# A two-layer streaming encoder step: norm weights applied on ScalarE, last tiles squared singly, two blocks normed before the SSM, roots by table

## The chip, the cores and the metric

One core of a Trainium2 chip runs one step of a small streaming encoder. The metric is the device time of one execution in microseconds (us), here the median of several runs. The core has a matrix engine (PE, TensorE, which reads SBUF and writes PSUM banks), three elementwise engines (DVE, VectorE; ACT, ScalarE, which looks its functions up in tables that it loads; POOL, GpSimd), and a sync engine (SP) that issues most DMAs in the order of its own queue. Each engine runs its instructions in order and waits at semaphores for the others.

## The reference

Two layers over T = 1088 tokens (1024 of a prompt, 64 of a sample), width 1024, fp32. Every block is sandwiched between norms, and this change is about them.

```python
def rms_norm(x, g):
    x32 = x.astype(jnp.float32)
    y = x32 * lax.rsqrt(jnp.mean(x32 * x32, axis=-1, keepdims=True) + NORM_EPS) * g.astype(jnp.float32)
...
def conv_ffn(h, prev, w_up, conv_w, conv_b, w_down):
    up = h @ w_up
    full = jnp.concatenate([prev.astype(up.dtype), up], axis=1)
    c = conv_b
    for j in range(CONV_WIDTH):
        c = c + conv_w[j] * full[:, j:j + t]
    y = (jax.nn.gelu(c[..., :D_FF]) * c[..., D_FF:]) @ w_down
...
    for i in range(DEPTH):
        hp = rms_norm(xp, g_pre_mix[i])
...
        xp = xp + rms_norm(mp, g_post_mix[i])
...
        hp = rms_norm(xp, g_pre_ffn[i])
...
        xp = xp + rms_norm(fp, g_post_ffn[i])
```

The mixer of layer 0 is windowed attention. That of layer 1 is an SSM: an input matrix, a complex diagonal scan over tokens, an output matrix, GELU, and a gated product (GLU).

## The kernel before

**Layout.** Activations lie transposed: 128 partitions, 8 k-tiles of the width, tokens along the free axis. The tokens are cut into blocks of 384, 384 and 320 (b = 0, 1, 2). A product of fp32 values is three matmuls (`mm3`, L181 to L183) of high and low halves: of the activations (`hh`, `hl`) and the weights (`whl`). Weights come by SP's DMA into `raw`, ACT rounds them to the high half (L175), DVE subtracts for the low half (L176), two units ahead of use.

**Stages.** Attention, FFN 0, SSM, FFN 1. Between them lie the joints, where a post norm adds to the residual and a pre norm makes the next input: J1 (post_norm 1, pre_norm 2), J3 (post_norm 3, SSM norm), J4 (post_norm 5, pre_norm 6) and the end, J5 (post_norm 7 and the output); J2 is where FFN 0 turns from up to down. Block 2 is last at each joint. J3 and J5 stand alone, since nothing else is left for PE; in J1 and J4 PE works on the up products of blocks 0 and 1 while block 2 is normed.

**A norm** (`rstd`, L186). ACT squares two k-tiles at a time (L196), DVE adds them up (L198) and folds the pair (L201), PE sums over partitions with a column of ones (L207). The root is either by ACT's Sqrt (L211), a reciprocal and one Newton step on DVE (L230 to L232), or, with `root` false (J4), a bit trick and three Newton steps on DVE (L217 to L232), because Sqrt needs another table than the stage's sigmoid. PE then transposes the factors into a broadcast row `pr` (L225). `post_norm` multiplies `y` by weight and `pr` in one instruction for each k-tile on DVE (L264) and adds the residual, two k-tiles at a time, on POOL or DVE (L266). `pre_norm` makes `hh` on ACT (L241), `hl` on DVE (L247) or for k = 3, 5, 7 on POOL (L245), and `rb` (L249), which scales the up products as they leave PSUM (L295).

**Up** has 88 units of one weight tile: a buffer `u` is taken from the pool `t4`, two of its columns copied from a cache (L286), filled from PSUM, two more columns kept (L300), and run through the width-3 convolution on ACT and DVE (L303 to L305). **Down** (`down`) holds four PSUM banks, one for each of four output tiles, and goes over k; ACT empties them (L392) or DVE adds them (L394).

**Into the SSM.** `ssm_bounce` copies the new residual into `xs` with tokens reordered by position in a chunk of 8 (L867, ACT); blocks 0 and 1 during down of block 2, block 2 in J3. The four quarters go to DRAM (`hd`, L873) and come back as `U` (L917), 16 channels of a group on the partitions. The factors of the norm are applied then, by DVE on `U` for all 137 columns (`ssm_scale`, L923): `ssm_norm` spreads them with small products (L902) into `rs`. The SSM runs over 32 pairs, `batch` after `batch`: PE forms inputs (L990), DVE multiplies and scans (L991 to L1013), PE forms outputs (L1028), ACT drains them (`ys`, L1032).

**What sets the order.** The program is written in tiles; a framework's scheduler, which simulates the program, puts the instructions of each engine in one fixed order, within the limits of tile pools and of explicit order constraints (`order`). So an edit can move instructions far from it.

## Time and profile before

| what | us |
|---|---|
| median of 3 runs | 2345.57 (2342.53 to 2351.72) |
| profiled execution | 2347.37 |
| its span in the trace | 2345.6 |
| PE busy | 2267.0 |
| DVE busy | 1460.2 |
| ACT busy | 893.7 |
| POOL busy | 277.5 |

The profiled execution is 1.8 us above the median, and its span is 1.8 us shorter than its own time. The timeline rows read: start in us from the span's start, busy us, engine, line and operation, outputs<-inputs, shape, count, and in brackets the idle time ahead of it with what ended it. A PE row merges pipelined matmuls.

### The profile page before, as it was taken

How to read it: one execution, taken by the hardware profiler on the slowest of the kernel's cores; microseconds unless marked ns; L12 is line 12 of the kernel's file. 1: busy time of each engine (PE TensorE's matmuls, PEld its weight loads, DVE VectorE, ACT ScalarE, POOL GpSimd, SP SyncE). 2: the span in 40 equal slices, each digit the busy share in tenths (PEclk: the TensorE clock that was granted, in tenths of full speed). 3: DMA queues.
4: the chain of work that ended last, by engine and by line, in shares of the span. 5: the costliest groups of instructions: out<-in, count | busy, mean ns of one | idle time of the engine just before them, and what ended most of it. 6: DMA issues, size and time to landing. Idle time of an engine off the chain costs nothing. (4 is left out here: it accounts for less than half of the span.)

```text
span 2345.6 us, 35751 instructions
## 1 busy us (share of the span) xinstructions
PE 2267.0 (97%) x14265; PEld 2197.5 (94%) x14265; DVE 1460.2 (62%) x2836; ACT 893.7 (38%) x1463; POOL 277.5 (12%) x286
## 2 busy tenths in 40 slices
PE   8999999999999999999968899999999999999997
PEld 7987799999999999999956799999999999999997
DVE  8677639898576766564649712587555555465554
ACT  5256645322233433443625621343222222254332
POOL 5222005000123221010000000240000000000000
PEclk9999999999999999999978899999999999999998
DMA  5000015312334344765567721242211221166652
GB/s 191 33 30 19 28 51 176 118 62 102 97 127 144 126 139 150 230 193 162 193 250 243 222 68 54 73 155 82 93 60 71 85 74 64 56 215 182 208 179 94
DMA packets 167958, 287.01 MB, mean 122 GB/s; under 512 B 22032, under 2 KB 104496, under 8 KB 167664
## 3 DMA queue, kind: packets, MB, share of 16 engines
q1 hardware_dynamic: 157440, 273.41, 35.8%
q0 software_dynamic: 2032, 6.83, 0.9%
q10 hardware_dynamic: 8320, 4.49, 0.8%
q8 instruction: 112, 1.84, 0.3%
q14 instruction: 54, 0.44, 0.1%
HBM read 214.52 MB, written 70.17 MB: 121 GB/s over the span
## 5 line engine op out<-in xcount | busy, mean ns | idle before, releaser
L181 PE MATMUL mm<-hl,whl 128*128 128x384 f32 (+1 forms) x2232 | 735.1, 330 | 16.0 <-DVE hl L247 7.5
L183 PE MATMUL mm<-hh,whl 128*128 128x384 f32 (+1 forms) x2232 | 733.4, 329 | 1.9 <-DVE whl L176 1.9
L182 PE MATMUL mm<-hh,whl 128*128 128x384 f32 (+1 forms) x2232 | 734.9, 329 | 0.0
L175 ACT ACTIVATE whl<-raw 128x1024 fp32r<-128x1024 f32 x256 | 269.9, 1058 | 709.6 <-PE mm L183 583.5
L176 DVE TENSOR_TENSOR whl<-raw,whl 128x1024 fp32r<-128x1024 f32 x256 | 320.7, 1255 | 232.5 <-ACT whl L175 229.7
L181 PEld LDWEIGHTS mm<-hl,whl 128*128 128x128 f32 x2232 | 420.3, 188 | 18.1 <-DVE hl L247 9.0
L183 PEld LDWEIGHTS mm<-hh,whl 128*128 128x128 f32 x2232 | 420.1, 188 | 2.8 <-DVE whl L176 2.7
L182 PEld LDWEIGHTS mm<-hh,whl 128*128 128x128 f32 x2232 | 420.5, 188 | 0.4
L181 PE MATMUL mm<-gt,whl 128*128 128x384 f32 (+1 forms) x1056 | 347.0, 329 | 3.6 <-ACT y L392 2.8
L182 PE MATMUL mm<-gt,whl 128*128 128x384 f32 (+1 forms) x1056 | 345.9, 328 | 0.0
L183 PE MATMUL mm<-gt,whl 128*128 128x384 f32 (+1 forms) x1056 | 343.1, 328 | 0.7 <-DVE whl L176 0.7
L295 DVE TENSOR_TENSOR u<-rb,mm 128x384 f32<-128x384 f32 (+1 forms) x264 | 131.8, 507 | 284.6 <-PE mm L183 283.5
L181 PEld LDWEIGHTS mm<-gt,whl 128*128 128x128 f32 x1056 | 198.7, 188 | 4.9 <-ACT y L392 3.4
L183 PEld LDWEIGHTS mm<-gt,whl 128*128 128x128 f32 x1056 | 198.3, 188 | 1.0 <-DVE whl L176 1.0
L182 PEld LDWEIGHTS mm<-gt,whl 128*128 128x128 f32 x1056 | 198.9, 188 | 0.0
L303 ACT ACTIVATE t<-u,ppt 128x1090 f32<-128x1090 f32 x88 | 113.4, 1289 | 29.3 <-DVE u L297 17.7
L304 DVE SCALAR_TENSOR_TENSOR t<-u,ppt,t 128x1090 f32<-128x1090 f32 x88 | 118.9, 1351 | 7.9 <-ACT t L303 7.9
L305 DVE SCALAR_TENSOR_TENSOR t<-u,ppt,t 128x1090 f32<-128x1090 f32 x88 | 118.9, 1351 | 1.7
L266 POOL TENSOR_TENSOR y<-y,xl 128x768 f32<-128x768 f32 (+1 forms) x18 | 32.3, 1801 | 624.6 <-DVE y L264 409.3
L318 ACT ACTIVATE t<-t 128x1090 f32<-128x1090 f32 x44 | 49.0, 1114 | 101.3 <-DVE t L305 101.3
L1085 DVE SCALAR_TENSOR_TENSOR y<-pa,ppt,sg 128x384 f32<-128x384 f32 (+1 forms) x24 | 14.1, 592 | 95.5 <-ACT sg L1084 95.5
L370 DVE TENSOR_TENSOR gt<-gr,gt 128x768 fp32r<-128x768 f32 (+2 forms) x70 | 57.9, 864 | 17.5 <-ACT gt L369 17.5
(315 smaller groups left out, 3279.1 us busy)
## 6 DMA issues: line engine op xcount, KB each, us to landing
raw<-in_w_down SPq DMA_DIRECT2D x132, 512.0 KB, 4.0
raw<-in_w_up SPq DMA_DIRECT2D x88, 512.0 KB, 3.3
gd<-t SPq DMA_DIRECT2D x44, 512.0 KB, 2.6
pm<-prm SPq DMA_DIRECT2D x32, 522.0 KB, 7.1
gr<-gd SPq DMA_DIRECT2D x28, 384.0 KB, 4.8
xl<-x SPq DMA_DIRECT2D x24, 384.0 KB, 4.0
raw<-in_w_glu SPq DMA_DIRECT2D x16, 512.0 KB, 4.4
gr<-gd SPq DMA_DIRECT2D x22, 320.0 KB, 4.6
```

The source lines that it names most:

```text
L175: nc.scalar.activation(w[:, 0], raw, AF.Copy)
L176: nc.vector.tensor_sub(w[:, 1], raw, w[:, 0].bitcast(F32))
L181: nc.tensor.matmul(out, w[:, 0, sl], xl, start=start, stop=False)
L182: nc.tensor.matmul(out, w[:, 0, sl], xh, start=False, stop=False)
L183: self.last_mm = nc.tensor.matmul(out, w[:, 1, sl], xh, start=False, stop=stop)
L266: by[q].tensor_add(y[:, 2 * q:2 * q + 2], y[:, 2 * q:2 * q + 2], xs[q])
L295: nc.vector.tensor_mul(u[:, t0 + 2:t0 + 2 + np_], rb[:, t0:t0 + np_], ps[:, :np_])
L303: nc.scalar.activation(t, u[:, 0:T + 2], AF.Identity, bias=cb(m), scale=cw(0, m))
L304: nc.vector.scalar_tensor_tensor(t, u[:, 1:T + 3], cw(1, m), t, op0=ALU.mult, op1=ALU.add)
L305: nc.vector.scalar_tensor_tensor(t, u[:, 2:T + 4], cw(2, m), t, op0=ALU.mult, op1=ALU.add)
L318: nc.scalar.activation(ta, ta, AF.Gelu_apprx_tanh)
L370: nc.vector.tensor_sub(x[:, 1, j:j + e], raw, x[:, 0, j:j + e].bitcast(F32))
```

## The change

Seven edits, all in the norms and what stands beside them:

1. `rstd` with `fine` (post norms of block 2): the last pair of k-tiles is squared and added one at a time, and the accumulator is folded before it.
2. `post_norm`: ACT scales `y` by the weight in eight activations (L269), ahead of the root; DVE multiplies pairs of k-tiles by `pr` (L277). Which engine adds the residual is a string, 0 for POOL and 1 for DVE: in block 2, "1111" for post_norm 3, "0101" for all others. In block 2 a product stays behind the DVE add ahead of it.
3. The roots of J4 come from the table for block 2 of post_norm 5 and blocks 1 and 2 of pre_norm 6.
4. The two small copies of each up unit go from DVE to ACT.
5. In `down`, the second half (mh = 1) of the first pass (c = 0) takes banks 0 and 1 for its first four k, and then banks 2 and 3.
6. The SSM norm of blocks 0 and 1 is applied before the bounce: `pr` is broadcast as in the other norms, kept in `rn`, and DVE multiplies in place of ACT's copy. `ssm_scale` covers only the 41 columns of block 2.
7. The order constraint of block 2's copies: the second copy stands behind the second square instead of the third.

```diff
--- before.py
+++ after.py
@@ -183,13 +183,20 @@
         self.last_mm = nc.tensor.matmul(out, w[:, 1, sl], xh, start=False, stop=stop)
 
 
-    def rstd(self, src, n, tag, root, bcast=True, first=False, alt=None, adder=None):
+    def rstd(self, src, n, tag, root, bcast=True, first=False, alt=None, adder=None, fine=False):
         nc = self.nc
         adder = adder or nc.vector
         acc = None
         for q in range(4):
             sq = self.n2(n, tag)
             xq = src[:, 2 * q:2 * q + 2]
+            if fine and q == 3:
+                adder.tensor_add(acc[:, 0], acc[:, 0], acc[:, 1])
+                for j in range(2):
+                    nc.scalar.activation(sq[:, j], xq[:, j], AF.Square)
+                    adder.tensor_add(acc[:, 0], acc[:, 0], sq[:, j])
+                break
             if first:
                 nc.gpsimd.tensor_mul(sq, xq, xq)
             else:
@@ -198,7 +205,8 @@
                 adder.tensor_add(acc, acc, sq)
             else:
                 acc = sq
-        self.summed = adder.tensor_add(acc[:, 0], acc[:, 0], acc[:, 1])
+        else:
+            adder.tensor_add(acc[:, 0], acc[:, 0], acc[:, 1])
         cuts = [min(c, n - P) for c in range(0, n, P)]
         nt = len(cuts)
         pr = self.sm_ps("pr", int(tag == "sqb") if alt is None else alt)
@@ -249,23 +257,31 @@
         nc.scalar.activation(rb[:, t0:t0 + n], pr[:, :n], AF.Copy)
         return hh, hl, r
 
-    def post_norm(self, y, b, g, xsrc, root, roomy, out=None):
+    def post_norm(self, y, b, g, xsrc, root, roomy, out=None, by=None):
 
         nc = self.nc
         n = BLK[b][1]
         xs = [self.t4([P, 2, n], "xl") if roomy and b == 2 else self.n2(n, "xl") for _ in range(4)]
         for q in range(4):
             nc.sync.dma_start(xs[q], xsrc[:, 2 * q:2 * q + 2])
-        pr, _ = self.rstd(y, n, "sqa", root, alt=b % 2 if roomy else None)
+        pr, _ = self.rstd(y, n, "sqa", root, alt=b % 2 if roomy else None, fine=b == 2)
+        for k in range(KD):
+            nc.scalar.activation(y[:, k], y[:, k], AF.Copy, scale=g[:, k:k + 1])
+        V, G = nc.vector, nc.gpsimd
+        by = [(G, V)[int(x)] for x in by or ("1001" if roomy and b == 2 else "0101")]
 
         def apply():
+            last = None
             for q in range(4):
-                for k in range(2 * q, 2 * q + 2):
-                    nc.vector.scalar_tensor_tensor(y[:, k], y[:, k], g[:, k:k + 1], pr[:, :n], op0=ALU.mult, op1=ALU.mult)
-                by = (nc.vector, nc.gpsimd, nc.gpsimd, nc.vector) if roomy and b == 2 else (nc.gpsimd, nc.vector) * 2
-                by[q].tensor_add(y[:, 2 * q:2 * q + 2], y[:, 2 * q:2 * q + 2], xs[q])
+                yq = y[:, 2 * q:2 * q + 2]
+                x = V.tensor_mul(yq, yq, pr[:, None, :n].to_broadcast([P, 2, n]))
+                if last is not None and b == 2:
+                    self.order(x, last)
+                x = by[q].tensor_add(yq, yq, xs[q])
+                if by[q] is V:
+                    last = x
                 if out is not None:
-                    nc.sync.dma_start(out[:, 2 * q:2 * q + 2], y[:, 2 * q:2 * q + 2])
+                    nc.sync.dma_start(out[:, 2 * q:2 * q + 2], yq)
         return apply
 
 
@@ -283,7 +299,7 @@
             u = self.t4([P, T + 4], "u")
             nc.vector.memset(u[:, 0:2], 0.0)
...
-            nc.vector.tensor_copy(u[:, SEQ + 2:SEQ + 4], self.pp[:, c0:c0 + 2])
+            nc.scalar.copy(u[:, SEQ + 2:SEQ + 4], self.pp[:, c0:c0 + 2])
...
 
...
@@ -297,8 +313,8 @@
                 nc.vector.tensor_mul(u[:, SEQ + 4:], rb[:, SEQ:], ps[:, np_:n])
 
         def conv(m, u):
-            nc.vector.tensor_copy(cst[:, m], bass.AP(tensor=u.tensor, offset=u[:, SEQ:SEQ + 2].offset,
-                                                     ap=[u.ap[0], [T + 2 - SEQ, 2], [1, 2]]))
+            nc.scalar.copy(cst[:, m], bass.AP(tensor=u.tensor, offset=u[:, SEQ:SEQ + 2].offset,
+                                                ap=[u.ap[0], [T + 2 - SEQ, 2], [1, 2]]))
             t = self.t4([P, T + 2], "t")
             nc.scalar.activation(t, u[:, 0:T + 2], AF.Identity, bias=cb(m), scale=cw(0, m))
             nc.vector.scalar_tensor_tensor(t, u[:, 1:T + 3], cw(1, m), t, op0=ALU.mult, op1=ALU.add)
@@ -380,6 +396,9 @@
                 ks = range(KCUT[c], KCUT[c + 1])
...
                 todo = [(k, m) for m in range(4) for k in ks] if ws else [(k, m) for k in ks for m in range(4)]
+                if c == 0 and mh == 1:
+                    todo = [(k, m) for u in ((0, 1), (2, 3)) for k in ks[:4] for m in u] + todo[16:]
                 for k, m in todo:
...
                         ws[k] = self.unit(("w_down", i, k, mh))
@@ -851,8 +870,7 @@
     def ssm_bounce(self, xt, b, qs=range(4), after=None):
 
         nc = self.nc
-        t0, n = BLK[b]
-        segs = [(0, n, 48 * b)] if b < 2 else [(0, 256, 96), (256, 320, 129)]
+        segs = [(0, 384, 48 * b)] if b < 2 else [(0, 256, 96), (256, 320, 129)]
         if b == 0:
             self.hw = {}
             self.hd = self.dram.tile([D, 8, NC_], F32, name="hd")
@@ -864,9 +882,14 @@
                 o = self.xs[q][:, :, :, c:c + (v - u) // 8]
...
-                x = nc.scalar.activation(o, xt[:, 2 * q:2 * q + 2, u:v].rearrange("p k (c s) -> p k c s", s=8), AF.Copy)
+                x = xt[:, 2 * q:2 * q + 2, u:v].rearrange("p k (c s) -> p k c s", s=8)
+                if b < 2:
+                    r = self.rn[:, 384 * b:384 * b + 384].rearrange("p (c s) -> p c s", s=8)
+                    nc.vector.tensor_mul(o, x, r[:, None].to_broadcast([P, 2, 48, 8]))
+                    continue
+                x = nc.scalar.activation(o, x, AF.Copy)
                 if after is not None:
-                    self.order(x, after[(0, 2, 3, 3)[q]])
+                    self.order(x, after[(0, 1, 3, 3)[q]])
             if b == 2:
...
@@ -882,29 +905,29 @@
 
         nc = self.nc
         n = BLK[b][1]
-        ps, r = self.rstd(xt, n, "sqa" if b == 2 else "sqb", True, bcast=False, alt=1 - b % 2, adder=nc.gpsimd if b == 0 else None)
+        ps, r = self.rstd(xt, n, "sqa" if b == 2 else "sqb", True, bcast=b < 2, alt=1 - b % 2, adder=nc.gpsimd if b == 0 else None)
         if b == 0:
...
-            sel = self.t4([P, 330], "sel")
-            self.lsel, self.dsel, self.ex, self.rs = sel[:, :128], sel[:, 128:144], sel[:, 144:192], sel[:, 192:329]
+            sel = self.t4([P, 1001], "sel")
+            self.lsel, self.dsel, self.ex, self.rs, self.rn = (sel[:, x:y] for x, y in ((0, 128), (128, 144), (144, 192), (192, 233), (233, 1001)))
...
-            nc.vector.memset(self.rs[:, 128:129], 0.0)
+            nc.vector.memset(self.rs[:, 32:33], 0.0)
+        if b < 2:
+            nc.scalar.activation(self.rn[:, 384 * b:384 * b + 384], ps[:, :n], AF.Copy)
+            return
         ex = self.ex
         for i, c in enumerate(range(0, n, P)):
...
-        if b < 2:
-            self.last_rs = nc.scalar.activation(self.rs[:, 48 * b:48 * b + 48], ps[:, :48], AF.Copy)
-        else:
-            nc.scalar.activation(self.rs[:, 96:128], ps[:, :32], AF.Copy)
-            self.last_rs = nc.scalar.activation(self.rs[:, 129:137], ps[:, 32:40], AF.Copy)
+        nc.scalar.activation(self.rs[:, 0:32], ps[:, :32], AF.Copy)
+        self.last_rs = nc.scalar.activation(self.rs[:, 33:41], ps[:, 32:40], AF.Copy)
 
     def ssm_load(self, q):
 
@@ -920,7 +943,9 @@
         return u
 
     def ssm_scale(self, u, x, y):
-        return self.nc.vector.tensor_mul(u[:, x:y], u[:, x:y], self.rs[:, None, :].to_broadcast([P, y - x, NC_]))
+        u = u[:, x:y, 96:]
+        return self.nc.vector.tensor_mul(u, u, self.rs[:, None, :].to_broadcast([P, y - x, 41]))
 
     def ssm(self, after):
         nc, tc, a = self.nc, self.tc, self.a
@@ -1194,7 +1219,8 @@
 
             def f(b, y):
                 ys.append(y)
-                c.post_norm(y, b, g(post), xs[b], post != 5, post in (3, 7), xo[b] if pre is None else None)()
+                c.post_norm(y, b, g(post), xs[b], post != 5 or b == 2, post in (3, 7), xo[b] if pre is None else None,
+                            {3: "1111", 7: "0101"}.get(post) if b == 2 else None)()
                 if pre == 4:
                     if b == 2:
                         c.ssm_bounce(y, b, [0])
@@ -1217,7 +1243,7 @@
             def second(b):
                 if b == 0:
                     rb.append(c.t4([P, T], "rb"))
-                nxt[b] = c.pre_norm(ys[b], b, g(pre), rb[0], pre != 6)
+                nxt[b] = c.pre_norm(ys[b], b, g(pre), rb[0], pre != 6 or b > 0)
             return f, nxt, rb, early
         f, n1, r1, _ = then(1, xin, cols(xd[0]), 2)
         c.attention(h, rb, f)
```

Three places in the engines' orders, as the scheduler puts them.

SP at J3, before: `pm` are SSM parameters, `hd<-xs` writes a quarter (the first as two halves), `U<-hd` reads one, and `x_91<-y` spills the residual.

```order
L937 DMA pm<-prm 128x1044 x12
L873 DMA hd<-xs 128x1096 x2
L917 DMA U<-hd 128x8x137
L873 DMA hd<-xs 128x2x1096 x2
L917 DMA U<-hd 128x8x137
L873 DMA hd<-xs 128x2x1096
L917 DMA U<-hd 128x8x137 x2
```

And SP at the same place with the change:

```order
L962 DMA pm<-prm 128x1044 x12
L896 DMA hd<-xs 128x1096 x2
L896 DMA hd<-xs 128x2x1096
L940 DMA U<-hd 128x8x137
L896 DMA hd<-xs 128x2x1096
L940 DMA U<-hd 128x8x137
L896 DMA hd<-xs 128x2x1096
L940 DMA U<-hd 128x8x137 x2
```

One whole quarter, the fourth, whose copy is the last on ACT, now stands ahead of the first `U` load; then loads and writes alternate.

PE in J4, before: the two transposes (L225, `nvsqa` of post_norm 5 block 2, then `nvsqb` of pre_norm 6 block 1) between up products of blocks 0 and 1 (128x384).

```order
L182 MATMUL mm<-hh,whl 128x384
L225 MATMUL pr<-ident,nvsqa 128x128 x3
L183 MATMUL mm<-hh,whl 128x384
L181 MATMUL mm<-hl,whl 128x384
L182 MATMUL mm<-hh,whl 128x384
L183 MATMUL mm<-hh,whl 128x384
L181 MATMUL mm<-hl,whl 128x384
L182 MATMUL mm<-hh,whl 128x384
L183 MATMUL mm<-hh,whl 128x384
L181 MATMUL mm<-hl,whl 128x384
L182 MATMUL mm<-hh,whl 128x384
L225 MATMUL pr<-ident,nvsqb 128x128 x3
```

And with the change, where the sums (L215) and transposes (L233) of the same norms stand:

```order
L183 MATMUL mm<-hh,whl 128x384
L215 MATMUL pr<-ones,sqb 128x1 x3
L181 MATMUL mm<-hl,whl 128x384
L182 MATMUL mm<-hh,whl 128x384
L183 MATMUL mm<-hh,whl 128x384
L181 MATMUL mm<-hl,whl 128x384
L233 MATMUL pr<-ident,nvsqa 128x128 x3
L182 MATMUL mm<-hh,whl 128x384
L183 MATMUL mm<-hh,whl 128x384
```

The transposes of post_norm 5 stand four products behind the second sum, where they stood 24 behind; counted from J4's first product, 109 products are ahead of them instead of 131. Those of pre_norm 6 stand 30 products behind them instead of 9.

DVE in J3, before, from the root's last step to the last fold of the SSM norm:

```order
L232 SCALAR_TENSOR_TENSOR nvsqa<-nvsqa 128x3
L264 SCALAR_TENSOR_TENSOR y<-y,ppt,pr 128x320 x8
L266 TENSOR_TENSOR y<-y,xl 128x640 x2
L198 TENSOR_TENSOR sqa<-sqa 128x640 x3
L201 TENSOR_TENSOR sqa<-sqa 128x320
```

And with the change:

```order
L277 TENSOR_TENSOR y<-y,pr 128x640
L280 TENSOR_TENSOR y<-y,xl 128x640
L277 TENSOR_TENSOR y<-y,pr 128x640
L280 TENSOR_TENSOR y<-y,xl 128x640
L277 TENSOR_TENSOR y<-y,pr 128x640
L280 TENSOR_TENSOR y<-y,xl 128x640
L277 TENSOR_TENSOR y<-y,pr 128x640
L205 TENSOR_TENSOR sqa<-sqa 128x640
L280 TENSOR_TENSOR y<-y,xl 128x640
L205 TENSOR_TENSOR sqa<-sqa 128x640 x2
L209 TENSOR_TENSOR sqa<-sqa 128x320
```

All products stood ahead of the two DVE adds (POOL had the others); now each product is followed by its add, and all four adds are DVE's.

## Prediction

> **What bounds the kernel now.** I read the head of the page first, then the idle time of TensorE by releaser, then the stretches where that idle time lies.
>
> ```profile
> span 2345.6 us, 35751 instructions
> PE 2267.0 (97%) x14265; PEld 2197.5 (94%) x14265; DVE 1460.2 (62%) x2836; ACT 893.7 (38%) x1463; POOL 277.5 (12%) x286
> PE pr L207 <- DVE sqa L201: 19.0, 3, 13.2
> PE mm L181 <- ACT whl L175: 8.2, 3, 7.4
> PE mm L181 <- DVE hl L247: 7.5, 3, 5.1
> PE p L1023 <- ACT ys L1032: 6.9, 4, 3.4
> PE p L1028 <- issue: 4.1, 1, 4.1
> PE mm L181 <- ACT y L392: 2.8, 2, 2.3
> ```
>
> TensorE (PE) is busy 97% of the span, and the change removes no matrix product. What can be won is PE's idle time, the slower clock behind it, and the tail after the last product. The rows (total, times, longest) name the owners: the sums of the post norms wait for VectorE (19.0 us in 3 waits), the FFNs wait for `hl` at the joints (7.5), the SSM for `ys` and for its own start (6.9 and 4.1). The change works on these. The 8.2 us before the first weights stay.
>
> **The end, J5 (post_norm 7, block 2): -1.6.**
>
> ```profile
> 2328.55 0.49 DVE L394 TENSOR_TENSOR y<-y,mm 128x320 f32<-128x320 f32 x1 [3.90 <-PE mm L183]
> 2329.13 0.74 ACT L196 ACTIVATE sqa<-y 128x640 f32<-128x640 f32 x1 [8.04 <-DVE y L394]
> 2329.90 0.82 DVE L198 TENSOR_TENSOR sqa<-sqa 128x640 f32<-128x640 f32 x1 [0.86 <-ACT sqa L196]
> 2330.76 0.49 DVE L201 TENSOR_TENSOR sqa<-sqa 128x320 f32<-128x320 f32 x1
> 2331.40 1.41 PE L207 MATMUL pr<-ones,sqa 128*128 128x1 f32 x6 [2.88 <-DVE sqa L201]
> 2334.97 3.75 DVE L264 SCALAR_TENSOR_TENSOR y<-y,ppt,pr 128x320 f32<-128x320 f32 x8 [1.00 <-PE pr L225]
> 2337.02 3.03 POOL L266 TENSOR_TENSOR y<-y,xl 128x640 f32<-128x640 f32 x2 [63.09 <-DVE y L264]
> 2338.64 2.82 DVE L266 TENSOR_TENSOR y<-y,xl 128x640 f32<-128x640 f32 x2
> ```
>
> After the last product come a pair squared (0.74), added (0.82), halves added (0.49). Now it is one tile: a square of 320 elements, which I estimate at 0.44 from the row of 640 (0.74, less 320 at about 0.95 ns), and one add of 0.49. The 2.05 becomes 0.93, so PE starts its sum 1.1 earlier. The weights' scaling on ACT lies beside DVE and PE and ends before the root needs ACT. Behind the root, eight STT (3.75) become four broadcast products of 640, each estimated at 0.82 (the row of L198), 3.3 in all. The two DVE adds spread over 2.82 because the first runs beside POOL; two alone would be about 1.6. The new order, two products, an add, two products, an add, still ends on an add beside POOL's second one. Bounds for this half: 0 (the lock stays) and -1.6 (both gains whole); the two rows are nearest to -0.5, since POOL's 3.03 stays on the path. Sum -1.6, range -1.1 to -2.7.
>
> **Into the SSM, J3: -1.0 up to the first SSM product.**
>
> ```profile
> 1205.99 3.76 DVE L264 SCALAR_TENSOR_TENSOR y<-y,ppt,pr 128x320 f32<-128x320 f32 x8 [1.00 <-PE pr L225]
> 1209.67 2.83 DVE L266 TENSOR_TENSOR y<-y,xl 128x640 f32<-128x640 f32 x2
> 1217.63 2.48 ACT L867 ACTIVATE xs<-y 128x512 f32<-128x512 f32 x4
> 1219.19 1.44 PE L207 MATMUL pr<-ones,sqa 128*128 128x1 f32 x6 [13.23 <-DVE sqa L201]
> 1224.54 0.72 PE L990 MATMUL p<-U,pm 128*64 128x137 f32 x4 [0.88 <-PE pr L902]
> 1196.67 7.93 SPq L937 DMA_DIRECT2D pm<-prm  x12
> 1213.16 0.79 SPq L873 DMA_DIRECT2D hd<-xs  x2
> 1216.13 0.37 SPq L917 DMA_DIRECT2D U<-hd  x1
> 1206.00:1228.00 22.00, 6.36 (x33) 5.22 (x33) 12.86 (x26) 9.54 (x21) 4.02 (x9) 0.50 0.99 366
> ```
>
> On DVE all eight products ran before the first add, so the first `xs` copy waited until about 1211.8. Now product and add alternate, each pair about 0.82 + 0.82 = 1.65, and start 1.15 earlier (fine squaring): the first quarter is ready at 1204.8 + 1.7 = 1206.5, the last at 1211.5. Behind that ACT does four squares (0.74) and the copies; its last copy ends near 1215.7, PE's sum falls to about 1214.6, and the scale `rs` to about 1219.5, 4.5 earlier. But SP's new order issues quarter 3 of `hd` ahead of the first `U` load. That load thus waits for ACT's last copy, and it lies behind 1.1 MB more. At the last row's 366 GB/s and a DMA share of 0.99, quarter 0 (1.1 MB, 3.0 us) follows the `pm` loads and is through by about 1217.4, quarter 3 by 1220.2, and `U` (0.55 MB, 1.5 us, with 1.5 allowed until it is seen) lands near 1223.2. First product 1223.5 against 1224.5: -1.0. Without that order it would be -4. This is my choice of the binding queue; bounds 0 and -4.5.
>
> **Inside the SSM: -5.5.**
>
> ```profile
> 1230.00:1330.00 100.00, 82.71 (x804) 68.01 (x802) 89.58 (x147) 61.68 (x179) 4.60 (x30) 0.86 0.81 248
> L923 DVE TENSOR_TENSOR U<-U,sel x9: 446/1273/1292, 1224.0 to 1303.2; 128x1096 f32<-128x1096 f32 x7, 128x274 f32<-128x274 f32 x1, 128x822 f32<-128x822 f32 x1
> 1234.78 1.54 PE L1028 MATMUL p<-wk,pm 64*128 64x137 f32 x14 [4.11 <-issue]
> ```
>
> DVE is the busiest engine here (89.58 of 100, PE 82.71 at a clock of 0.86). The nine scalings shrink from 137 to 41 columns: seven go from 1.27 to an estimated 0.50 (446 ns at 274 elements and 1273 at 1096 give about 1.0 ns an element; 328 elements now). That is 7 x 0.77 = 5.4 of DVE. Where DVE ends last, all of it counts; where PE or ACT does, nothing. PE comes within 7 of DVE, so I take two thirds, -3.5. The start has the 4.11 gap, in which DVE had a 1.29 scaling ahead of the chain; the scaling and the new order by pairs save some 2 of it. Bounds 0 and -9. The price is paid in down of block 2: eight bounces go from ACT to DVE as products of 768, about 1 us each by the 0.82 for 640. DVE has room there (62% busy overall), so nothing.
>
> **J4 (post_norm 5, pre_norm 6): -5.3.**
>
> ```profile
> 1553.63 0.16 DVE L232 SCALAR_TENSOR_TENSOR nvsqb<-nvsqb 128x3 f32<-128x3 f32 x1
> 1555.55 0.49 PE L225 MATMUL pr<-ident,nvsqa 128*128 128x128 f32 x3
> 1556.08 3.76 DVE L264 SCALAR_TENSOR_TENSOR y<-y,ppt,pr 128x320 f32<-128x320 f32 x8 [2.28 <-PE pr L225]
> 1563.77 0.63 PE L181 MATMUL mm<-hl,whl 128*128 128x320 f32 x1 [5.10 <-DVE hl L247]
> 1563.00:1567.00 4.00, 3.23 (x12) 3.24 (x13) 4.00 (x5) 1.73 (x3) 3.81 (x4) 0.57 0.02 7
> 343.78 1.28 ACT L211 ACT_TABLE_LOAD   x1
> ```
>
> The norm was ready long before PE reached the transposes at 1555.55: their place in PE's order bound. They now stand 22 products earlier, at 0.16 us each (2267.0 over 14265) 3.5: the broadcast is ready at about 1552.5, `hl` of k 0 after a product, an add, `hh` and `hl` (0.82 twice, and twice 0.47 as one of the eight in 3.76) at 1555, and PE reaches block 2 at about 1558. The gap of 5.10 goes, and about 1.2 at a clock of 0.57 behind it, less 1.0 for k 3 to 6, whose adds are POOL's. The table root replaces the bit trick, but needs a table load, 1.28 in the row of the first layer, while the sums are still on the way. What it takes back is hidden as long as ACT has no cast due in those microseconds. Bounds -6.3 and -2 (late `hl` of the POOL quarters).
>
> The Trainium skill, "ScalarE: Activation LUTs", section "What ACT_TABLE_LOAD costs", speaks against this step: every switch costs the load and a drain, 2.66 us by its figure. The row shows the load of the same 1.28 and no drain beside it. By the page's price the chain in J4 would lose 1.4 and the step come to -3.9; by the row it stays -5.3.
>
> **J1 and J2: -2.7 and -0.9.**
>
> ```profile
> PE mm L181 <- DVE hl L247: 2.4, 2, 1.2
> PE mm L181 <- POOL hl L245: 1.1, 2, 0.6
> 954.39 1.06 ACT L175 ACTIVATE whl<-raw 128x1024 fp32r<-128x1024 f32 x1 [1.78 <-DMA raw<-in_w_down]
> 955.35 1.61 ACT L392 ACTIVATE y<-mm 128x384 f32<-128x384 f32 x4
> ```
>
> From 380 to 412 PE waited 2.4 + 1.1 for `hl`. The products of blocks 1 and 2 now cost DVE less, and the broadcasts come 3 to 6 products earlier in PE's order: I take 2.7 of 3.5, bounds 0 and -3.5. In J2 PE waited 2.3 for a bank that ACT emptied at 955.35, behind a cast whose weights came by DMA. The reordered `todo` asks for two banks first, but the cast at 954.39 stays in front: -0.9, bounds 0 and -2.3.
>
> **Extra work:** blocks 0 and 1 now need six transposes for the SSM norm in place of six small products, +0.5 on PE. The 176 small copies moved to ACT, 0.16 each on DVE, lie beside the products: 0.
>
> **Sum.** -1.6 - 1.0 - 5.5 - 5.3 - 2.7 - 0.9 + 0.5 = -16.5. The profiled execution took 2347.4 (span 2345.6), so 2330.9; the median shown, 2345.6, is 1.8 lower, which gives 2329.1. I say **2330**.
>
> **The rivals.**
>
> *The middle stays as it is.* DMA is at 0.99 in J3, and everything the SSM starts with passes through it; after the start PE and ACT run nearly as full as DVE. Then J3 and the SSM give -1 instead of -6.5, and J1 nothing. 2347.4 - 16.5 + 5.5 + 2.7 = 2339, or 2337 by the median. For it: the clock of 0.50 and 0.86 comes from waits that the change leaves. Against: DVE is busiest. Within 0.5%.
>
> *The joints don't move.* The change says that norms get off DVE; if the POOL adds still lock DVE out (a DVE add of 0.82 took 2.1 beside POOL in J5) and `hl` of the POOL quarters comes late, J1 and J4 keep their gaps: 2.7 + 4.3 less, 2337, by the median 2335 or a little more. With the first rival 2343. The Trainium skill, "SBUF — State Buffer", section "Who interferes with whom", gives the lock as exclusive for a DVE operation with two SBUF operands against a reading POOL: the product from PSUM would be free of it, the adds not. The 2.82 for two adds agrees.
>
> *Slower: ACT holds up the weights.*
>
> ```profile
> L175 ACT ACTIVATE whl<-raw 128x1024 fp32r<-128x1024 f32 x256 | 269.9, 1058 | 709.6 <-PE mm L183 583.5
> L286 DVE COPY u<-ppt x88: 154/162/1802, 394.5 to 2061.7; 128x2 f32<-128x2 f32 x88
> ```
>
> Every weight passes an ACT cast that PE itself releases. The copy into a fresh `u` waits for its slot (1802 ns once, on DVE); on ACT such a wait stands in front of a cast. If each of 88 units lost 0.3 us, that is +26, net +10: 2357, by the median 2355. It decides when the wait exceeds ACT's slack: a unit takes PE about 12 us (72 products at 0.16) and ACT's cast 1.06 of it. With ACT idle 583 us in wait for PE ahead of its casts, that is unlikely.
>
> **How the numbers follow.** Forecast (2322 to 2333) 0.52; middle stays 0.22; joints don't move 0.14, a third of it both together; slower 0.06; more than summed, under 2322 (the start at -4, the whole of DVE's 5.4, J5 -2.7: 2319) 0.06. The range, 2318 to 2341, leaves out the slow rival, part of the combined one and the far ends of the bounds. About 0.5%, 11.7 us, is what a measurement of this kernel can tell from no change, so faster means below 2333.8: forecast and better, 0.58, and a part of the others, 0.03: **0.61**; within 0.33; slower 0.06.
>
> **What would show it.** Right: no wait for `hl` above 1 us in J4; first SSM product near 1223.5, with the `U` load as its last releaser and `rs` ready 4 us before; the scalings near 0.5 and DVE below 85 of 100; the output adds ending near 2323. Wrong: an ACT cast as releaser of PE inside the up stages; the SSM as long as before with PE waiting for `ys`; a second stretch of clock below 0.7 in J4. It fails as a whole if the weights' DMA sets the pace somewhere that PE's lateness now hides.

## The result, and the profile after

The changed kernel takes 2329.92 us (median of 4 runs, 2328.51 to 2331.38) against 2347.78 (4 runs, 2342.53 to 2351.72): a ratio of 0.9925, 95% interval 0.9903 to 0.9948, or 17.9 us less. The forecast was 2330. In the profiled execution the span fell by 17.0, from 2345.6 to 2328.6. The head of the page after, and TensorE's idle time by releaser:

```profile
span 2328.6 us, 35802 instructions
PE 2262.8 (97%) x14259; PEld 2194.2 (94%) x14259; DVE 1437.8 (62%) x2596; ACT 948.4 (41%) x1735; POOL 281.6 (12%) x284
PE p L1048 <- ACT ys L1057: 11.1, 3, 4.2
PE pr L215 <- DVE sqa L209: 10.6, 2, 10.2
PE mm L181 <- ACT whl L175: 8.2, 2, 7.2
PE p L1015 <- DVE U L948: 4.4, 1, 4.4
PE pr L215 <- DVE sqa L198: 3.4, 2, 1.7
PE mm L181 <- ACT y L411: 1.8, 2, 1.5
PE mm L181 <- DVE hl L255: 1.4, 2, 1.0
```

The waits for `hl` (7.5 before) fell to 1.4, those of the post norms' sums fell from 19.0 to 14.0, and a new one (4.4, for `U`) and a longer one (`ys`, 11.1 for 6.9) took back a part.

Here a product is one matmul instruction. The 11568 products that write `mm`, `pa` and `pb` all stand in every trace, in nearly the same order, so the starts of the n-th product (counted from 0) cut the program into stages. The table gives the length of each stage in us (J1: products 900 to 1160; J2: 4230 to 4300; down: 4300 to 5616, which is FFN 0's down from J2 on, but for its last 48 products; J3: to the first product with `U`; SSM: from there to product 5850; J4: 6900 to 7100; end: from product 11567 to the span's end). The last column but one is the other stages together. Each of e1 to e10 is a single profiled run; e11 and e12 were timed four times each.

| kernel | J1 | J2 | down | J3 | SSM | J4 | end | others | span |
|---|---|---|---|---|---|---|---|---|---|
| before | 52.36 | 16.35 | 224.66 | 31.56 | 144.36 | 42.04 | 17.39 | 1816.88 | 2345.6 |
| changed | 50.85 | 12.88 | 227.59 | 30.88 | 140.18 | 36.17 | 14.68 | 1815.37 | 2328.6 |
| e12, changed again | 50.71 | 12.26 | 226.87 | 30.88 | 139.58 | 36.27 | 14.52 | 1816.57 | 2327.7 |
| e1, norm late | 50.71 | 13.70 | 225.93 | 31.22 | 140.45 | 36.16 | 14.52 | 1817.11 | 2329.8 |
| e2, banks together | 50.76 | 15.99 | 225.83 | 31.34 | 136.14 | 36.12 | 14.24 | 1816.78 | 2327.2 |
| e3, bit trick | 50.62 | 12.56 | 225.93 | 30.93 | 140.48 | 37.00 | 14.17 | 1816.71 | 2328.4 |
| e4, quarter 3 last | 50.64 | 13.15 | 226.01 | 28.82 | 146.38 | 36.16 | 14.14 | 1815.30 | 2330.6 |
| e5, weights on DVE | 50.82 | 12.40 | 227.88 | 30.78 | 139.86 | 39.85 | 14.89 | 1817.41 | 2333.9 |
| e6, copies on DVE | 50.00 | 13.30 | 226.53 | 31.90 | 138.67 | 36.18 | 14.17 | 1815.61 | 2326.4 |
| e7, z later | 50.98 | 12.49 | 226.07 | 28.89 | 151.36 | 36.18 | 14.76 | 1815.49 | 2336.2 |
| e8, GLU weight early | 50.84 | 12.76 | 226.70 | 28.65 | 140.83 | 36.16 | 14.16 | 1815.65 | 2325.8 |
| e9, only banks | 52.56 | 13.11 | 224.28 | 31.75 | 144.00 | 43.01 | 16.78 | 1817.01 | 2342.5 |
| e10, only norm early | 52.53 | 14.27 | 227.98 | 31.99 | 144.66 | 44.60 | 16.77 | 1815.70 | 2348.5 |
| e11, combined | 50.54 | 12.28 | 226.62 | 28.96 | 140.77 | 36.27 | 13.52 | 1815.82 | 2324.8 |

Against before, the changed kernel gained 1.5 in J1, 3.5 in J2, 0.7 in J3, 4.2 in the SSM, 5.9 in J4 and 2.7 at the end, and lost 2.9 in down. The other stages gave 1.5 more; in e12, the same kernel again, they gave 0.3.

The largest surprise is J2. The wait of TensorE there and a window of 3 us behind it, before and then after. A window row gives the busy time of PE, of its weight loads, of DVE, ACT and POOL, each with its instructions, then the granted TensorE clock, the DMA share and GB/s:

```profile
955.88 0.69 PE L181 MATMUL mm<-gt,whl 128*128 128x384 f32 x1 [2.33 <-ACT y L392]
956.00:959.00 3.00, 3.00 (x10) 3.00 (x11) 0.70 (x1) 0.96 (x3) 0.00 (x0) 0.50 1.06 400
```

```profile
953.72 0.44 PE L181 MATMUL mm<-gt,whl 128*128 128x384 f32 x1 [0.34 <-ACT y L411]
952.00:955.00 3.00, 2.66 (x15) 2.34 (x14) 1.23 (x1) 2.58 (x5) 0.00 (x0) 1.00 1.04 386
```

The stage was 3.5 longer with the gap of 2.33: behind it the clock stood at 0.50 for 3 us, and only 10 products ran in that window, where 15 ran in the window of the changed kernel. In the kernel before, it is product 4238 that waits for the bank, in the changed kernel product 4248. The ten products in between take 1.75 us at the 0.175 from start to start that the traces show there at full clock, while ACT's cast stands where it stood (2.42 us behind the start of product 4230, now 2.19).

At the end, TensorE, DVE and POOL of the changed kernel:

```profile
2315.93 0.93 PE L215 MATMUL pr<-ones,sqa 128*128 128x1 f32 x6 [1.70 <-DVE sqa L198]
2319.01 1.55 DVE L277 TENSOR_TENSOR y<-y,pr 128x640 f32<-128x640 f32 x2 [0.99 <-PE pr L233]
2319.97 1.54 POOL L280 TENSOR_TENSOR y<-y,xl 128x640 f32<-128x640 f32 x1 [57.61 <-DVE y L277]
2320.60 1.59 DVE L280 TENSOR_TENSOR y<-y,xl 128x640 f32<-128x640 f32 x1
2323.68 1.59 DVE L280 TENSOR_TENSOR y<-y,xl 128x640 f32<-128x640 f32 x1
```

The wait for the sum fell from 2.88 to 1.70, as computed, and the sum itself from 1.41 to 0.93. Each DVE add takes 1.59 beside POOL's, where the same add in J3, without POOL, took 0.82.

At J3, DVE, SP and TensorE of the changed kernel:

```profile
1204.79 0.82 DVE L280 TENSOR_TENSOR y<-y,xl 128x640 f32<-128x640 f32 x1
1205.43 8.44 SPq L896 DMA_DIRECT2D hd<-xs  x3
1213.98 0.41 SPq L940 DMA_DIRECT2D U<-hd  x1
1212.51 1.44 PE L215 MATMUL pr<-ones,sqa 128*128 128x1 f32 x6 [10.21 <-DVE sqa L209]
1221.04 0.57 DVE L948 TENSOR_TENSOR U<-U,sel 128x82 f32<-128x82 f32 x2 [5.39 <-DMA U<-hd]
1221.39 1.18 PE L1015 MATMUL p<-U,pm 128*64 128x137 f32 x8 [4.41 <-DVE U L948]
```

PE's sum came 6.7 earlier than before, but the first `U` load only 2.1 (issued at 1213.98, behind three writes of `hd`), and DVE waited 5.4 us for it to land.

In down the whole loss lies in block 2: from product 4300 to 5136, in blocks 0 and 1, the kernels differ by less than 0.4, and from 5136 to 5616 it is 76.10 before and 79.39 after. That stretch, before and after, and the three longest of TensorE's waits in it after:

```profile
1116.90:1193.00 76.10, 73.94 (x503) 72.63 (x502) 44.71 (x64) 41.13 (x49) 4.77 (x5) 1.00 0.53 169
1111.10:1190.50 79.40, 74.08 (x500) 72.27 (x499) 54.16 (x64) 35.67 (x51) 4.15 (x5) 1.00 0.51 162
PE mm L181 <- ACT y L411: 1.5, 1, 1.5
PE pr L215 <- DVE sqb L209: 1.1, 1, 1.1
PE mm L181 <- ACT whl L175: 1.0, 1, 1.0
```

DVE has 9.5 us more to do there, and TensorE's waits add up to 5.3 us for 2.1 before: 2.3 for the norms' own sums and roots (0.6 before), 1.5 for a PSUM bank that ACT empties (none before), and 1.5 for weights, as before.

In J1 one wait for `hl` of 0.95 is left of four (1.24, 1.18, 0.56 and 0.52). TensorE in the changed kernel, and 3.4 us of its clock; then the clock at the same place in e12, and a wait that only e12 has of the two:

```profile
401.11 0.41 PE L181 MATMUL mm<-hl,whl 128*128 128x320 f32 x1 [0.95 <-DVE hl L255]
401.60:405.00 3.40, 3.40 (x15) 3.40 (x14) 3.37 (x5) 1.28 (x3) 3.30 (x3) 0.50 0.18 63
```

```profile
402.80:406.20 3.40, 3.40 (x24) 3.21 (x23) 3.37 (x5) 1.28 (x3) 3.30 (x3) 1.00 0.14 52
408.41 0.54 PE L233 MATMUL pr<-ident,nvsqb 128*128 128x128 f32 x3 [0.98 <-DVE nvsqb L240]
```

### The profile page after: what moved, and what is told of

Its sections match the earlier page's. It is cut to its first block, busy times and chain, and to the rows that moved or that the text cites. A ratio compares the mean times of both kernels' runs of the same rounds, so it can differ in the third digit from the quotient of the medians.

```text
span 2328.6 us, 35802 instructions
## 1 busy us (share of the span) xinstructions
PE 2262.8 (97%) x14259; PEld 2194.2 (94%) x14259; DVE 1437.8 (62%) x2596; ACT 948.4 (41%) x1735; POOL 281.6 (12%) x284
## 4 chain that ended last, share of the span: by engine, by line
PE 49%; DMA 4%; DVE 3%; ACT 2%; issue 1%; POOL 0%; SPq 0%; ACTq 0%; DVEq 0%; POOLq 0%
PE mm L181 13%; PE mm L183 13%; PE mm L182 13%; DMA raw<-in_w_down 2%; PE pb L181 1%; PE pb L183 1%; PE pb L182 1%; PE pa L182 1%; PE pa L183 1%; PE pa L181 1%; DMA yd<-ys 1%; DVE whl L176 1%; DVE y L277 0%; ACT whl L175 0%; DMA gr<-gd 0%
```

## The experiments

The question after the result: the sum was right, but were the terms? J2 and down both lie far from theirs. All differences below are of the stages in the table. "The theory" and "the rival" are those of the expectation quoted with each run.

**e1.** Edit 6 undone.

```diff
-                if b < 2:
-                    r = self.rn[:, 384 * b:384 * b + 384].rearrange("p (c s) -> p c s", s=8)
-                    nc.vector.tensor_mul(o, x, r[:, None].to_broadcast([P, 2, 48, 8]))
-                    continue
...
-        u = u[:, x:y, 96:]
-        return self.nc.vector.tensor_mul(u, u, self.rs[:, None, :].to_broadcast([P, y - x, 41]))
+        return self.nc.vector.tensor_mul(u[:, x:y], u[:, x:y], self.rs[:, None, :].to_broadcast([P, y - x, NC_]))
```

> The changed kernel without edit 6: blocks 0 and 1 are bounced by ACT un-normed, and all 137 columns of U are scaled in the SSM, as before the change. Theory: the eight products of the bounce on DVE and the two more sums and transposes are what cost 3.5 us in down of block 2, so the last product of FFN 0 comes 3 to 3.5 earlier than in the changed kernel, and the smaller scalings are what gained inside the SSM, so the stretch from the first SSM product to the GLU gets 3 to 5 longer; the total within 1.5 of the changed kernel. Rival 1: down lost its 3.5 to something else (weight casts, the copies on ACT); then its end stays within 1. Rival 2: the SSM's gain came from the start (order by pairs), not from the scalings; then the SSM gets less than 1 longer and the total is 3 better than the changed kernel.

Measured: down 225.93, 0.9 to 1.7 less than the two profiles of the changed kernel and 1.3 more than before. But e2, e3, e4 and e7, which keep edit 6, took 225.83 to 226.07 there, so this run does not show that edit 6 costs anything in the changed kernel, and the theory is not borne out. The SSM took 140.45, as with the small scalings (140.18 and 139.58): rival 2 is right there, as far as one profile tells, though the total did not get 3 better.

**e2.** Edit 5 undone.

```diff
-                if c == 0 and mh == 1:
-                    todo = [(k, m) for u in ((0, 1), (2, 3)) for k in ks[:4] for m in u] + todo[16:]
```

> The changed kernel without edit 5: down goes over all four banks for each k again. Theory: the order of banks is what took away the wait at J2, and the slow clock behind it: the wait of 2.3 for y comes back, some 8 products behind it take 0.32 in place of 0.18 us, 3 to 3.6 us in all, and nothing else moves. Rival: the wait shrank because ACT and DVE have other work ahead (edits 2 and 4); then J2 stays within 0.5.

Measured: J2 15.99, 3.1 longer, as the theory had it: the wait came back with 1.91, again before product 4238, and the slow clock behind it. But the kernel was not slower in all (span 2327.2): its SSM took 136.14, 4.0 less, with the same order of instructions there. No edit accounts for that; I take it for the spread of single profiles, which e12 sizes below.

**e3.** Edit 3 undone.

```diff
-                c.post_norm(y, b, g(post), xs[b], post != 5 or b == 2, post in (3, 7), xo[b] if pre is None else None,
+                c.post_norm(y, b, g(post), xs[b], post != 5, post in (3, 7), xo[b] if pre is None else None,
-                nxt[b] = c.pre_norm(ys[b], b, g(pre), rb[0], pre != 6 or b > 0)
+                nxt[b] = c.pre_norm(ys[b], b, g(pre), rb[0], pre != 6)
```

> The changed kernel without edit 3: the roots in J4 by shift and three Newton steps on DVE, no table load there. Theory: the root's length set where the transposes stand in TensorE's order; with it back they stand some 20 products later, and 4 to 6 us come back at J4 (a gap of 3 to 5 and a slow clock behind it). Rival: the products with the broadcast and the weights on ACT freed DVE, and the root did little; then J4 gets at most 2 longer. If the table's loads cost ACT anything that TensorE waits for, something would get shorter, in J4 or in the first up units behind it, by up to 1.4.

Measured: J4 37.00, 0.8 longer: the rival. The transposes now stand behind 118 products of J4's up, 9 later than in the changed kernel, not 20. The load of the table and the root, and the transposes of post_norm 5, in the changed kernel:

```profile
1540.10 1.28 ACT L219 ACT_TABLE_LOAD   x1
1541.39 0.26 ACT L219 ACTIVATE nvsqa<-pr,eps 128x3 f32<-128x3 f32 x1
1544.06 0.49 PE L233 MATMUL pr<-ident,nvsqa 128*128 128x128 f32 x3
```

And the transposes here, with the wait of block 2's first product:

```profile
1544.64 0.49 PE L233 MATMUL pr<-ident,nvsqa 128*128 128x128 f32 x3
1550.99 0.42 PE L181 MATMUL mm<-hl,whl 128*128 128x320 f32 x1 [0.94 <-DVE hl L255]
```

J4 starts 1.0 us earlier here, so the transposes came 1.6 later than with the table; block 2 waited 0.94, and no slow clock followed.

**e4.** One more order constraint.

```diff
             self.order(self.hw[2], self.last_u)
+            self.order(self.hw[3], self.last_u)
```

> The changed kernel with one more order constraint: the write of the fourth quarter of hd stands behind both loads of U's first tile on SP, where it stood ahead. Theory: the load's place in the queue is what holds the first SSM product; the scale is ready at 1217.2, so the first product comes near 1218.0 in place of 1221.4 (3.0 to 3.5 earlier). Of that the SSM keeps 1 to 3, since ys and DVE set its pace later. Rival: the DMA engines are full there (share 1.0) and the first quarter's write lands no earlier; then the first product comes less than 1 earlier, and the total stays.

Measured: J3 28.82, the first product at 1217.7, as the theory had it. But the SSM took 146.38, 6.2 more, and the total was no better. The waits of TensorE and ACT in this SSM (total, times, longest), and ACT's stop at the GLU's first weight:

```profile
PE p L1049 <- ACT ys L1058: 15.1, 3, 7.0
ACT whl L175 <- DMA raw<-in_w_glu: 4.9, 1, 4.9
ACT z L1074 <- DMA yf<-yd: 3.6, 2, 2.7
1305.62 0.43 ACT L1058 ACTIVATE ys<-p 128x137 f32<-128x137 f32 x2
1310.99 1.06 ACT L175 ACTIVATE whl<-raw 128x1024 fp32r<-128x1024 f32 x1 [4.93 <-DMA raw<-in_w_glu]
1311.95 2.04 ACT L1074 ACTIVATE z<-yf 128x1024 f32<-128x1024 f32 x1
```

The earlier start ran into ACT's queue: at its head the cast of the GLU's first weight waits for a DMA, behind it stand a GELU and the `ys` that TensorE needs.

**e5.** Edit 2's scaling undone, its adds kept.

```diff
-        for k in range(KD):
-            nc.scalar.activation(y[:, k], y[:, k], AF.Copy, scale=g[:, k:k + 1])
...
-                x = V.tensor_mul(yq, yq, pr[:, None, :n].to_broadcast([P, 2, n]))
+                for k in range(2 * q, 2 * q + 2):
+                    x = V.scalar_tensor_tensor(y[:, k], y[:, k], g[:, k:k + 1], pr[:, :n], op0=ALU.mult, op1=ALU.mult)
```

> The changed kernel without the weights on ACT: eight STT with weight and broadcast on DVE for each block again, as before the change; adds, fine squares, roots and all else stay changed. Theory: after the table root turned out to be worth 0.8 us, the gain of J4 is that of the products: two k-tiles are ready 1.6 us after the broadcast and the rest beside the adds. Then J4 gets 3 to 5 longer, J1 1 to 1.5, and J5 0.5 to 1. Second question: every run with the change loses 1.3 to 3 us in down of block 2 against before, also without the early norms; if the scalings of blocks 0 and 1 on ACT, ahead of the casts there, are the cause, this run loses less than 0.7. Rival: the sum stands earlier (fine squares, first sum 1.9 earlier) and that alone moved the transposes; then J4 gets less than 1.5 longer.

Measured: J4 39.85, 3.7 longer: the theory. The transposes stand behind 124 products there, 109 in the changed kernel, and block 2 waits:

```profile
1553.79 0.42 PE L181 MATMUL mm<-hl,whl 128*128 128x320 f32 x1 [2.11 <-DVE hl L255]
1554.10:1557.40 3.30, 3.30 (x13) 3.30 (x12) 3.30 (x5) 1.02 (x2) 3.20 (x3) 0.50 0.02 6
```

J1 did not move (50.82), and the end got 0.2 to 0.4 longer, so the theory missed both. Down is as long as ever (227.88), so nothing here says that the scalings on ACT are what it lost.

**e6.** Edit 4 undone.

```diff
-            nc.scalar.copy(u[:, SEQ + 2:SEQ + 4], self.pp[:, c0:c0 + 2])
+            nc.vector.tensor_copy(u[:, SEQ + 2:SEQ + 4], self.pp[:, c0:c0 + 2])
...
-            nc.scalar.copy(cst[:, m], bass.AP(tensor=u.tensor, offset=u[:, SEQ:SEQ + 2].offset,
+            nc.vector.tensor_copy(cst[:, m], bass.AP(tensor=u.tensor, offset=u[:, SEQ:SEQ + 2].offset,
```

> The changed kernel with the two small copies of each up unit on DVE again. Theory: they lie beside the products on either engine; the up stages keep their length within 0.1 us from unit to unit, and the total stays within 1.5. Rival (the slower case of the prediction): on ACT they stood in front of the casts; then up gets shorter by more than 1 in each FFN.

Measured: from J1 to J2 529.82 us (529.79 changed, 529.93 before), and in the second FFN's up, products 7100 to 9900, 462.15 in all three: the copies cost and gain nothing there. J1 was 0.7 to 0.9 shorter; in e11, which has the same edit, it was 0.2 to 0.3 shorter.

**e7.** e4, and a step between `yf` and its GELU.

```diff
                     if kt < 7:
                         yield
                         yield
+                        yield
                     z = self.t4([P, T], "z")
```

> The kernel of e4 (fourth quarter behind U's loads, first SSM product at 1217.7) with one step more between the load of yf and its GELU in the SSM's pipeline, so that ACT empties ys before it takes up the GELU. Theory: what ate the earlier start in e4 is ACT's queue: the GELU waits for yf (2.7 at the first) with ys queued behind, and TensorE stands 6.0 and 7.0 for ys. Then the waits for ys halve at least, and the GLU's products come 3 to 6 earlier than in e4. Rival: the transfers themselves set the pace (yf and the GLU's weights land no earlier whatever ACT does); then ACT and TensorE wait elsewhere, and the GLU comes within 1.5 of e4.

Measured: the rival, and worse. The SSM took 151.36, 5.0 more than e4; ACT now stood 10.3 us for a transfer of `yd`, and the waits for `ys` did not halve:

```profile
ACT L1075 <- DMA yd<-ys: 10.3, 1, 10.3
PE p L1049 <- ACT ys L1058: 9.5, 3, 8.9
```

**e8.** e4, and the first GLU weight ahead of the fifth `yf` on SP; for that its load is asked for in an earlier batch (the one that ends with pair 29, in place of 31).

```diff
-                if qs[-1] == 31:
+                if qs[-1] == 29:
...
                         self.order(self.loaded, got[15])
+                        if j == 0:
+                            self.order(yfs[4], self.loaded)
```

> The kernel of e4 with the first weight of the GLU loaded ahead of the fifth yf on SP, where it stood behind. Theory: the second long wait for ys in e4 (7.0) is the cast of that weight at the head of ACT's queue, idle 4.9 for its DMA; SP issues that DMA only after a yf load that itself waits for ys. Then the cast finds its weight, that wait falls below 3, and the GLU comes 3 to 5 earlier than in e4; the first wait (6.0, for yf) stays. Rival: the weight's DMA waits for a buffer or for the full queue; then it lands at the same time and nothing changes.

Measured: SSM 140.83, 5.5 less than e4, so that the earlier start was kept; of the 15.1 us of waits for `ys`, 6.6 are left, one of them the first (5.5):

```profile
PE p L1052 <- ACT ys L1061: 6.6, 3, 5.5
1307.94 1.05 ACT L175 ACTIVATE whl<-raw 128x1024 fp32r<-128x1024 f32 x1
```

The cast waits for no DMA in that row, as the theory had it.

**e9.** The kernel before, and the two lines shown in e2 added to it.

> The kernel before with edit 5 alone. Theory: the order of banks is worth 3.1 us at J2 by itself (16.35 us between products 4230 and 4300 in the kernel before), and the stretch from there to the end of FFN 0's down then loses 1 to 1.5 of it again, because the weights' loads, not TensorE, set the pace in down of block 2; the total is 1.5 to 2.5 better than before. Rival: the loss of 1.3 to 3 in down, seen in every run with the change, comes from the change's other edits; then down keeps its 224.7 us within 0.5 and all of the 3.1 stays.

Measured: J2 13.11 (3.2 gained), down 224.28, nothing given back: the rival. So what down lost comes from other edits.

**e10.** The kernel before with edit 6 (the diff of e1 the other way, the norm of `ssm_norm` with it).

> The kernel before with edit 6 alone: blocks 0 and 1 normed in down, 41 columns scaled in the SSM. Theory, as the prediction had it: the smaller scalings shorten the SSM by 3 to 4 us (from 144.4 between its first product and the GLU's 150th). Rival, from e1: what ends last there are transfers and the order on ACT; then the SSM gets shorter by less than 1.5. The eight products on DVE cost down of block 2 between 0.3 and 2.

Measured: the SSM 144.66 (144.36 before), down 227.98 (224.66 before). The rival, and 3.3 us of cost in down, more than expected; a part of it is the clock, which stood at 0.51 from 1182.9 to 1189.8, where the kernel before has no slow stretch in down. J4 (44.60) and J2 (14.27) moved too, which edit 6 doesn't touch. In J2 the gap was 1.73 and no slow clock followed it; in J4 a wait of 1.34 came on top, and the slow clock lasted 6.8 us for 3.4 before. The bounce products in the changed kernel:

```profile
L888 DVE TENSOR_TENSOR xs<-y,sel x8: 1557/1632/1662, 1098.8 to 1170.5; 128x768 f32<-128x768 f32 x8
```

And the busy time in 100 us of the SSM here (DVE is the third number):

```profile
1231.30:1331.30 100.00, 79.78 (x822) 65.73 (x824) 84.92 (x147) 60.00 (x177) 4.57 (x30) 0.91 0.80 248
```

DVE's 89.58 fell to 84.92, as the smaller scalings should make it, and the stage is as long as it was.

**e11.** The changed kernel with the edits of e4, e6 and e8, and "0011" in place of "0101" in post_norm 7.

> The changed kernel with four edits more: the fourth quarter's write behind U's loads, the first GLU weight ahead of the fifth yf (both as in e8), the small copies on DVE (as in e6), and at the end POOL adding the first two quarters and DVE the last two. Theory: the SSM ends 2 to 3 earlier than in the changed kernel, J1 0.8 earlier, and the end comes 0.6 to 1.2 earlier, since POOL's adds lie beside DVE's products, which read PSUM and are not held up, and DVE's adds start when POOL's are done: 3 to 5 us below the changed kernel in all. Rival: a new order in the SSM eats it; within 1 of the changed kernel.

Measured, 3 rounds: 2326.39 us (2324.40 to 2327.34), ratio to before 0.9893 (0.9873 to 0.9913). That is 2.4 below e12 beside it, a little less than expected; all its four runs lie below all four of e12. Against e12's profile J3 gave 1.9, the end 1.0, and J1 0.2; the SSM took 1.2 back. POOL and DVE at the end:

```profile
2317.18 3.61 POOL L280 TENSOR_TENSOR y<-y,xl 128x640 f32<-128x640 f32 x2 [57.49 <-DVE y L277]
2318.54 0.85 DVE L280 TENSOR_TENSOR y<-y,xl 128x640 f32<-128x640 f32 x1
2320.16 1.31 DVE L280 TENSOR_TENSOR y<-y,xl 128x640 f32<-128x640 f32 x1
```

DVE ends at 2321.5, 5.3 behind its first product, where it took 6.3 in the changed kernel.

**e12.** The changed kernel again.

> The changed kernel once more, unchanged, as the measure of what one profile can tell: its stages J2, J4 and J5 should repeat within 0.3 us; down of block 2 (2.9 lost in the first profile) and the SSM, where transfers set the pace, may differ by 1 to 3.

Measured: 2328.81 us (2327.74 to 2329.70), ratio 0.9905 (0.9889 to 0.9921). J4 and the end repeat within 0.2, J2 within 0.6 (more than expected), down and the SSM within 0.8. With e2, e3 and e6, whose instructions stand in the same order in the SSM, one order there took 136.1 to 140.5. With e3, e4 and e7, which have the same order in down, one order there took 225.9 to 227.6.

## Why the prediction was right, and where it was right by chance

The total came out at the forecast in part by luck, because misses of both signs cancelled. Changes against before, from the first profile and from e12:

| step | forecast | measured |
|---|---|---|
| J5 | -1.6 | -2.7, -2.9 |
| J3 | -1.0 | -0.7, -0.7 |
| SSM | -5.5 | -4.2, -4.8 |
| J4 | -5.3 | -5.9, -5.8 |
| J1 | -2.7 | -1.5, -1.7 |
| J2 | -0.9 | -3.5, -4.1 |
| down, with the extra work | +0.5 | +2.9, +2.2 |
| other stages | 0 | -1.5, -0.3 |

**J2 was mis-sized twice.** The prediction held that the cast in front would stay, and it did. But with ten products more to run before it needs the bank, TensorE lost nearly all of the wait (2.33 to 0.34), not 0.9 of it. And the prediction priced no slow clock there: 1.3 came on top because nine products at half clock went. e2 and e9 show that the order of banks did it, with and without the rest. The measured 3.5 lies outside the bounds of that term.

**Down was the step that failed.** "DVE has room there, so nothing" is wrong twice. A bounce product takes 1.63, not 1 us: it reorders 768 elements as ACT's copy did, and no faster. And room on DVE did not make the work free: DVE is busy 54 of 79 us in block 2, and still TensorE's waits there grew from 2.1 to 5.3, most of all for norm sums and roots that DVE makes and for a bank that ACT empties. By itself edit 6 cost 3.3 (e10). What it costs within the whole change is not shown: e1, without it, took as long in down as four runs with it (225.93 against 225.83 to 226.07), and the 1.3 that e1 lost against before is within the 1.7 by which runs of one order differ there. Which edit of the change costs what in down stays open; it is not the order of banks (e9).

**The SSM gained for another reason.** Four runs make a square: the order in which DVE and TensorE begin the SSM is the old one in before and e10, and finishes pair by pair in e1 and the changed kernel; the scalings have 137 columns in before and e1, 41 in e10 and the changed kernel. With the old order the SSM took 144.4 and 144.7, with the new 140.5 and 140.2. The difference of 4 lies at the start: the first product with `wk`, which forms the SSM's outputs, starts 10.2 us behind the first product with `U` before and 9.6 behind it in e10, but 5.7 in e1 and 6.5 in the changed kernel:

```profile
1227.87 0.51 PE L1053 MATMUL p<-wk,pm 64*128 64x137 f32 x4
```

The gap at the start, 4.1 us before, in which the prediction saw 2, is gone in both kernels with the new order (3.3 in e10). The 5 us of DVE's work that the scalings lost show no gain in either pair, but runs of one order differ by up to 4.4, so a smaller gain isn't ruled out. Being busiest is not being last. That the order is the cause is argued from where the time lies, since the new order came with the rest of the change; which edit turned the scheduler is not isolated. It is not 6, nor 5 (e9 has the old order).

**J4 gained as forecast, by products rather than by the root.** Of 5.9, the weights on ACT with the four broadcast products account for 3.7 (e5) and the table root for 0.8 (e3); the rest was not separated. "Their place in PE's order bound" holds: 109 products stand ahead of the transposes in the changed kernel, 118 with the bit trick back (e3), 124 with the weights back on DVE (e5) and 131 before, and the root was through 1.5 us before PE reached them in the changed kernel, 1.6 in e3, 3.5 in e5 and 3.4 before. Of the price that the Trainium skill gives for a switch of tables ("ScalarE: Activation LUTs", "What ACT_TABLE_LOAD costs"), the drain does not appear: the load took 1.28, and the root started 0.01 behind it. The load itself was not hidden behind the sums, as the prediction had it, since it began 0.3 after the sum; it cost nothing because PE came 1.5 later still.

**J1 gave less than forecast.** A wait for `hl` of 0.95 was left, and TensorE now waits for a norm's own sum (0.48) and root (0.98, in e12), where it did not before. In the first profile the slow clock held TensorE up until the root was ready, in place of that wait. The prediction counted sums and broadcasts that come earlier in PE's order as a gain alone; here PE then came to some of them before they were ready.

**J3's queue was read rightly.** `U`'s load behind the write of the fourth quarter held the first product at 1221.4 with the scale ready at 1217.3; without that write ahead (e4) 2.1 more came, of the 3 that were priced. What the prediction did not ask is what the SSM would do with an earlier start: in e4 it lost 6.2, and it kept the start only when e8 had moved the weight's load.

**J5** gained 1.2 by the single squares, as computed; 0.5 by a sum at a better clock, not priced; and 1.0 behind the root, within its bounds. POOL's adds still held DVE's: 1.59 against 0.82. e11 took some of that back by giving DVE its adds last. The sign "output adds ending near 2323" did not fit the prediction's own sum: they ended at 2341.5 before, and 16.5 less is 2325.0; they ended at 2325.3.

**The slower rival** (ACT holding up the weights) did not come: both up stages kept their length to 0.2 us.

## What to carry to other kernels

Before pricing work taken off the busiest engine, follow the waits of the stage to the queue that ends last; here an in-order ACT queue, with a cast at its head that waited for a DMA, ate an earlier start whole until the DMA was issued earlier. When you price a gap of TensorE, ask what the clock does behind it. And where a scheduler places instructions, an edit's largest effect may be an order elsewhere: two runs, the edit alone and the change without it, tell the two apart.

## What the runs showed of the hardware

Behind the gap of 2.33 us in J2 the clock stood at 0.50 for 3 us, and products of 128x384 started every 0.32 us there, every 0.175 at full clock. The length of a gap alone doesn't tell whether that happens: a gap of 1.73 at the same place (e10) and gaps of 1.24 and 1.18 in J1 before had no slow clock behind them, while one of 0.95 in J1 had it in the changed kernel's first profile and not in e12. In the clock records of all fourteen traces the slow stretches, but for the one that the span's end cuts off, last 3.41 us or a whole multiple of it, and all that a trace has begin on one grid of 3.41 us, which lies differently from run to run. So it seems to matter where on the grid a gap falls; no run here tests that.

A DVE product of 768 elements with reordered output takes 1.63 us, where ACT's copy of the same took 1.6 to 1.7 and a plain add of 640 takes 0.82. Beside POOL's add of 1.54, a DVE add of 640 takes 1.59.

Profiles with one order of instructions differ by up to 4.4 us in the SSM and by 1.7 in down, so a single profile can't settle less than that there; J4 repeated within 0.2.
